# A decoder block's first stage: loading x first, and the modulation weights in four column quarters with projection weights between

## The chip, the cores and the metric

The kernel runs on one core of one Trainium2 chip. The metric is the time of one launch in microseconds (us) as the device takes it. All rows below are from one profiled execution, which took 1054.42 us; its trace spans 1052.4 us of them.

## What is computed

One layer of a hybrid decoder on 512 tokens of width 1024, in float32. Only its first lines matter here:

```python
ada = jax.nn.silu(c) @ w_ada + b_ada                 # c: 1024, w_ada: 1024 x 6144
shift1, scale1, gate1, shift2, scale2, gate2 = split(ada, 6)
h = rms_norm(x, norm1_g) * (1 + scale1) + shift1     # x: 512 x 1024
proj = h @ w_in                                      # 1024 x 3656, the columns in groups
```

From `proj` come a gated short convolution and a sparse attention with an indexer, then an output projection, and then a mixture of 64 experts over the 512 tokens, which takes most of the time.

## The kernel before, in words

The program is written out in the order in which each engine takes its instructions; nothing reorders them afterwards. An engine that waits holds up everything behind it.

**Shift and scale.** They need columns 0 to 2047 of `w_ada`, 8 MB, as eight row chunks k of 128 rows. `load_wa` (L114) puts row chunk k with all 2048 columns, 1 MB, into one of six buffers R0 to R5; the eighth comes in two column halves (`load_wa_half`, L124). `ada1(k)` (L185) is VectorE's product of one such chunk: `acc1 += wa[k] * silu(c)[k]`, 128x2048, so eight of them make the whole sum over this axis. TensorE then sums `acc1` over the partitions, 128 columns at a time (L356), and gives columns of shift and scale.

**x.** Four token blocks b of 128 tokens (0.5 MB each) are loaded in turn with the weight chunks. `norm1_sq` and `norm1` (L248, L253) run on ScalarE (square with sum, scaling) and TensorE (transposes, L260), with two copies by ScalarE (L83) per block, and leave x transposed in `xnT`, in eight chunks k of 128 columns by 512 tokens.

**Modulation.** `modulate(k0, n)` (L352) does it for n chunks: TensorE's L356 on `acc1`, three small sums on VectorE (L357, L358, L360), then for each chunk ScalarE writes `hh` (the rounded high part, L363), VectorE the full value into `xnT` (L364) and the low part `hl` (L365).

**Projection.** The loop over steps i (L1060) goes through 7 groups of 512 columns by 8 chunks k. A weight tile of a step, 128x512, is split by `split(i)` (L323) in two: ScalarE writes the high part into a `ring` tile (L83), VectorE the low part (L315). Each step then has three matmuls (L86 to L88) for each of four banks. In group 0 the first bank is left out, and `kw_mm` (L498) puts three products of a further weight, `kws`, in its place. `raw` tiles of 512 KB (two steps each) are loaded six steps ahead, and steps are split three ahead (`LOOK`). The fourth buffer of `raw` is one half of a tile named `both`.

**What runs beside it.** The other four parts of `ada` are summed on the way by `ada_item` (L388): a 512 KB chunk of `w_ada` (`both`, `adaw`) is scaled by ScalarE (L83, 128x1024) and added by POOL (L396). One is due at steps 1, 2, 4, 6, 8 and so on. `rope_tables` (L195) makes small tables for the positions, and its first instruction converts the positions to float (`posf`, L196). `at(i, f)` (L472, called from L947 on) puts f ahead of step i.

All large loads are issued by SP in program order. Each waits until the load eight before it has landed, and until its buffer has been read.

Of the kernel before, what the change touches and what calls it, by code (L numbers as in the profile page):

```python
# [13 lines left out]
F32R = mybir.dt.float32r  # L14
# [3 lines left out]
OP = mybir.AluOpType  # L18
# [32 lines left out]
def build(tc, a, out):  # L51
    nc = tc.nc
    root = ExitStack()
    with root:
# [12 lines left out]
        def M(tag, shape, name, dt=F32):  # L67
            return mem.tile(shape, dt, name=name, tag=tag)
# [33 lines left out]
        posi = M("q1", [NB, P], "posi", I32)  # L102
# [5 lines left out]

        wada = a["w_ada"][0].rearrange("(k p) n -> p k n", p=P)
        xv = x2d.rearrange("(b p) d -> p b d", p=P)  # L110
        wa = []
        xt = [M("A6", [P, 2, D], "xt0"), M("A7", [P, 2, D], "xt1")]

        def load_wa(k):  # L114
            t = M(f"R{k % 6}", [P, 2 * D], f"wa{k}")
            if k < KC - 1:
                nc.sync.dma_start(t, wada[:, k, 0:2 * D])
            wa.append(t)

        def wa_half(t, g):  # L120

            return t.rearrange("p (a d) -> p a d", a=2)[:, :, 512 * g:512 * g + 512]

        def load_wa_half(g):  # L124
            nc.sync.dma_start(wa_half(wa[KC - 1], g), wa_half(wada[:, KC - 1, 0:2 * D], g))

        def load_x(b):
            nc.sync.dma_start(xt[b // 2][:, b % 2], xv[:, b])

        for b in range(NB):  # L130
            load_wa(b)
            load_x(b)
        for k in (4, 5):
            load_wa(k)
        nc.scalar.dma_start(svR[16:32], a["b_ada"][:, 0:2 * D].rearrange("o (k p) -> (o k) p", p=P))
        nc.scalar.dma_start(svR[8:16], a["norm1_g"].rearrange("o (k p) -> (o k) p", p=P))
        nc.scalar.dma_start(svR[32:44], a["conv_w"].rearrange("o i (k p) -> (o i k) p", p=P))
# [34 lines left out]
        sc = small(KC)  # L172
# [12 lines left out]
        def ada1(k, g=None):  # L185
            if k == 0:
                nc.vector.tensor_scalar(acc1, wa[k], sc[:, 0:1], None, op0=OP.mult)
            else:
                v = [wa[k], acc1] if g is None else [wa_half(t, g) for t in (wa[k], acc1)]
                nc.vector.scalar_tensor_tensor(v[1], v[0], sc[:, k:k + 1], v[1], op0=OP.mult, op1=OP.add)  # L190


        posf = M("q0", [NB, P], "posf")

        def rope_tables():  # L195
            nc.vector.tensor_copy(posf, posi)  # L196
            nc.tensor.transpose(K6[:, 0, :NB], posf, ident[:NB, :NB])
            posT = small(NB)
            nc.vector.tensor_copy(posT, K6[:, 0, :NB])
# [63 lines left out]
        ada1(0)
        ada1(1)
        load_wa(6)
        load_wa(7)
        load_wa_half(0)
        norm1_sq(0)
        for b in range(NB):
            if b + 1 < NB:  # L270
                norm1_sq(b + 1)
            norm1(b)
            ada1(b + 2)
            if b == 1:
                vectors()
        sin = cos = None

        def rope_build():
# [62 lines left out]
        ada1(7, 0)
        split(0)

        def split_kw():
            kwf = [t.rearrange("p k n -> p (k n)") for t in (kwr, kws[:, 0], kws[:, 1])]
            copy_a(kwf[1], kwf[0])
            nc.gpsimd.tensor_tensor(kwf[2], kwf[0], kwf[1], op=OP.subtract)
# [17 lines left out]
                nc.vector.tensor_sub(l, x, h)  # L365

        modulate(0, 1)
        ada1(7, 1)
        split(1)
        modulate(1, 3)  # L370
        split(2)
        split_kw()


        acc2 = M("B1", [P, 2, D], "acc2")
# [96 lines left out]
        def at(i, f, *args):  # L472
            hooks.setdefault(i, []).append((f, args))
# [470 lines left out]
            mods7 = M("A7", [P, 2, D], "mods7")  # L944
            bcast_rows(mods7[:, 1], a["norm2_g"], D)

        at(1, modulate, 4, 2)  # L947
        at(4, rope_build)
        at(2, modulate, 6, 2)
        at(8, qi_done)  # L950
        at(8, kw_done)
        at(9, kw_T)
# [107 lines left out]
        for i in range(NS):  # L1060
            for f, args in hooks.pop(i, []):
                f(*args)
            g, k = divmod(i, KC)
            if i + 6 < 8 * NG:
                load_step(i + 6)
            if g < NG:
                split_step(i + LOOK if i + LOOK < 8 * NG else NS)
# [8 lines left out]
            if g < NG:  # L1076
                t = splits.pop(i)
                for j in range(4):
                    fill(i, r + (1.2 if j == 0 and k == 0 else 0))
                    if g == 0 and j == 0:  # L1080
                        for kk in {0: (), 1: (), 7: (5, 6, 7)}.get(k, (k - 2,)):
                            kw_mm(kk)
                    elif g < 4:
                        mm3(banks[j], hh[k // 4][:, k % 4, j * P:(j + 1) * P], hl[k // 4][:, k % 4, j * P:(j + 1) * P],
                            t[:, 0], t[:, 1], k == 0, k == KC - 1)
                    else:
                        mm3(banks[j], t[:, 0, j * P:(j + 1) * P], t[:, 1, j * P:(j + 1) * P], hh[k // 4][:, k % 4],
                            hl[k // 4][:, k % 4], k == 0, k == KC - 1)
# [885 lines left out]
```

## Time and profile before

| what | us |
|---|---|
| median of 3 runs (1052.13 to 1064.34) | 1053.35 |
| the profiled execution | 1054.42 |
| its span in the trace | 1052.4 |
| TensorE busy | 912.7 |
| VectorE busy | 531.4 |
| ScalarE busy | 270.5 |
| POOL busy | 391.6 |

The change touches about the first 75 us. There the trace is read by stretches (which engine is busy), then by the instructions of one engine in order of time, each with the idle time before it and what ended that.

### The profile page before, as it was taken

The numbers are of one execution on the slowest core, as the hardware profiler recorded it, in microseconds if no ns is written. First come the engines' busy times: TensorE is split into PE (matmuls) and PEld (weight loads), VectorE is DVE, ScalarE is ACT, GpSimd is POOL, SyncE is SP. The second block draws the span as 40 slices with busy tenths as digits, with TensorE's granted clock in tenths as the row PEclk, the third lists the DMA queues.
The fourth block names the chain that finished last, engine by engine and source line by source line (L and its number), as shares of the span: only waits on it lengthen the run. The fifth ranks groups of instructions, "written<-read, shape, count | busy, mean of one in ns | idle before, by whom it ended". The sixth has DMA issues, their size and how long they took to land. (4 is left out here: it accounts for less than half of the span.)

```text
span 1052.4 us, 14840 instructions
## 1 busy us (share of the span) xinstructions
PE 912.7 (87%) x4156; PEld 535.2 (51%) x4157; DVE 531.4 (50%) x1299; ACT 270.5 (26%) x527; POOL 391.6 (37%) x402
## 2 busy tenths in 40 slices
PE   1788989899998889788999989999998888889883
PEld 1666556566666767554444434444444444444341
DVE  4865976677756887734233434333233333333331
ACT  4544545544354442020000101111111111111110
POOL 3254688443534555332122323223232323333331
PEclk9989989899999989999999999999999999999987
DMA  9544232332523766695699996888988788889621
GB/s 336 196 162 158 88 128 86 121 100 80 180 92 109 278 223 230 202 329 177 195 298 317 278 346 229 286 274 297 308 293 301 260 288 267 294 258 373 158 33 27
DMA packets 71288, 227.80 MB, mean 216 GB/s; under 512 B 11858, under 2 KB 13010, under 8 KB 70208
## 3 DMA queue, kind: packets, MB, share of 16 engines
q1 hardware_dynamic: 55512, 189.90, 50.3%
q0 software_dynamic: 15520, 35.72, 14.9%
q8 instruction: 80, 1.31, 0.5%
q14 instruction: 104, 0.85, 0.2%
q10 hardware_dynamic: 72, 0.02, 0.0%
HBM read 207.75 MB, written 27.39 MB: 223 GB/s over the span
## 5 line engine op out<-in xcount | busy, mean ns | idle before, releaser
L1715 PE MATMUL pAB<-w,xT 128*128 128x512 f32 (+2 forms) x928 | 300.2, 609 | 18.8 <-ACTq L1878 5.7
L1715 PEld LDWEIGHTS pAB<-w,xT 128*128 128x128 f32 (+2 forms) x928 | 122.9, 160 | 154.0 <-issue 133.1
L1167 POOL DMA_INDIRECT out_dram<-ysb,misc x38 | 60.8, 1599 | 210.9 <-DVE ysb L1161 98.5
L1782 PE MATMUL pY<-w,q2u 128*128 128x512 f32 x256 | 116.4, 598 | 5.8 <-issue 4.1
L83 ACT ACTIVATE xT<-pX 128x512 f32<-128x512 f32 x59 | 35.1, 596 | 207.7 <-PE pX L1661 207.6
L1469 POOL DMA_INDIRECT X<-h_d,misc x51 | 54.2, 1063 | 84.6 <-DVE misc L1443 32.2
L1167 POOL DMA_INDIRECT out_dram<-y,misc x20 | 31.7, 1585 | 131.6 <-DMA out_dram<-ysb,misc 28.8
L1161 DVE SCALAR_TENSOR_TENSOR ysb<-pY,misc,gate 128x512 f32<-128x512 f32 x56 | 39.5, 746 | 70.7 <-DMA out_dram<-ysb,misc 31.7
L1782 PEld LDWEIGHTS pY<-w,q2u 128*128 128x128 f32 x256 | 46.5, 192 | 53.9 <-issue 51.9
L1454 DVE TENSOR_REDUCE rd<-pI 128x4 f32<-128x12 f32 (+1 forms) x45 | 7.6, 168 | 118.7 <-PE pI L1451 118.6
L315 POOL TENSOR_TENSOR ring<-raw,ring 128x512 fp32r<-128x512 f32 x29 | 38.4, 1323 | 70.2 <-ACT ring L83 70.2
L86 PE MATMUL Z<-ring,hh 128*128 128x512 f32 x120 | 56.3, 469 | 0.0
L87 PE MATMUL Z<-ring,hh 128*128 128x512 f32 x120 | 50.9, 424 | 0.0
L88 PE MATMUL Z<-ring,hl 128*128 128x512 f32 x120 | 50.9, 424 | 0.0
L396 POOL TENSOR_TENSOR acc<-acc,both 128x1024 f32<-128x1024 f32 x16 | 38.4, 2401 | 32.1 <-ACT both L83 22.7
L83 ACT ACTIVATE ring<-raw 128x512 fp32r<-128x512 f32 x66 | 41.3, 627 | 34.1 <-PE Z L88 30.3
L315 DVE TENSOR_TENSOR ring<-raw,ring 128x512 fp32r<-128x512 f32 x37 | 41.3, 1124 | 17.3 <-ACT ring L83 15.7
L86 PE MATMUL Z<-hh,ring 128*128 128x512 f32 x96 | 44.5, 463 | 0.0
L396 POOL TENSOR_TENSOR acc<-acc,adaw 128x1024 f32<-128x1024 f32 x16 | 39.1, 2446 | 14.1 <-DVE cy L629 7.5
L1788 PE MATMUL pY<-w,q2u 128*32 128x256 f32 (+1 forms) x360 | 33.9, 419 | 11.2 <-issue 8.0
L1446 DVE TENSOR_SCALAR gts<-sl,pu 128x256 bf16<-128x256 bf16 x180 | 41.5, 301 | 1.6
L1661 PE MATMUL pX<-ident,X 128*128 128x128 f32 x268 | 40.6, 289 | 0.0
(452 smaller groups left out, 1600.9 us busy)
## 6 DMA issues: line engine op xcount, KB each, us to landing
w<-in_w_dram SPq DMA_DIRECT2D x164, 512.0 KB
w<-in_w_dram SPq DMA_DIRECT2D x41, 1024.0 KB
raw<-in_w_in_dram SPq DMA_DIRECT2D x21, 512.0 KB
both<-in_w_ada_dram SPq DMA_DIRECT2D x16, 512.0 KB
adaw<-in_w_ada_dram SPq DMA_DIRECT2D x16, 512.0 KB
wa<-in_w_ada_dram SPq DMA_DIRECT2D x7, 1024.0 KB
raw<-in_w_out_dram SPq DMA_DIRECT2D x12, 512.0 KB
both<-in_w_in_dram SPq DMA_DIRECT2D x7, 512.0 KB
```

The lines of the kernel that those rows point to most:

```text
L83: nc.scalar.activation(o, i, AF.Copy, **kw)
L86: nc.tensor.matmul(p, lh, rh, start=start, stop=False)
L87: nc.tensor.matmul(p, lh, rl, start=False, stop=False)
L88: nc.tensor.matmul(p, ll, rh, start=False, stop=stop)
L315: eng.tensor_tensor(t[:, 1], r, t[:, 0], op=OP.subtract)
L396: eng.tensor_tensor(t, t, w, op=OP.add)
L1167: nc.gpsimd.indirect_dma_start(out=parts(acc_d, k), out_offset=bass.IndirectOffsetOnAxis(ap=idx, axis=0), in_=y[:, 0:D // k], in_offset=No ...
L1446: nc.vector.tensor_scalar(selx[:, b], sl2, pu[:, b, u:u + 1], None, op0=OP.is_equal)
L1469: nc.gpsimd.indirect_dma_start(out=xg[:, 0:D // k], out_offset=None, in_=parts(h2_d, k), in_offset=bass.IndirectOffsetOnAxis(ap=idx, axis= ...
L1661: nc.tensor.transpose(pX[c // 4][:, c % 4], x[:, c * P:(c + 1) * P], ident)
L1715: nc.tensor.matmul(ab[r * m:r * m + r], x[:, c, r * m:r * m + r], slot(v, cw // 4)[:, :, cw % 4], start=c == 0, stop=c == KC // k - 1)
L1782: nc.tensor.matmul(pY[n], q2[:, i, c], slot(w, 2)[:, c, 512 * n:512 * n + 512], start=c == 0, stop=c == 1)
```

## The change

x is loaded ahead of all weights. The 8 MB of shift and scale are cut by columns: `load_wa(g)` loads quarter g, that is 256 columns of shift and the 256 of scale that belong to them, for all eight row chunks, in eight loads of 256 KB with rows of 1 KB. `ada1(g)` is then eight products of 128x512, and after it chunks 2g and 2g+1 can be modulated. The weights of `kws` are loaded after quarter 1 was used (`load_kw`), in a buffer that quarter 1 had, and split at step 4; their products move to steps 5 to 7. `posf` is converted at the start, and `rope_build` moves from step 4 to step 6.

```diff
-        for b in range(NB):
-            load_wa(b)
-            load_x(b)
-        for k in (4, 5):
-            load_wa(k)
+        def load_wa(g):
+            for n in range(4 * g, 4 * g + 4):
+                if n % 2 == 0:
+                    t = M(f"R{n // 2 % 6}", [P, 2, 2, 2, 256], f"wa{n}")
+                    wa[n], wa[n + 1] = t[:, 0], t[:, 1]
+                for i in range(2):
+                    nc.sync.dma_start(wa[n][:, i], quarter(wada[:, 2 * (n % 4) + i, 0:2 * D], g))
+        for b in range(NB):
+            nc.sync.dma_start(xt[b // 2][:, b % 2], xv[:, b])
+        load_wa(0)
...
+        def ada1(g):
+            t = quarter(acc1, g)
+            for k in range(KC):
+                w = wa[4 * g + k // 2][:, k % 2]
+                if k == 0:
+                    nc.vector.tensor_scalar(t, w, sc[:, 0:1], None, op0=OP.mult)
+                else:
+                    nc.vector.scalar_tensor_tensor(t, w, sc[:, k:k + 1], t, op0=OP.mult, op1=OP.add)
+        nc.vector.tensor_copy(posf, posi)
...
         load_ahead(0)
-        load_wa_half(1)
-        nc.sync.dma_start(kwr, win[:, :, 3584:3656])
-        for i in range(2, 6, 2):
-            load_ahead(i)
-        ada1(6)
-        ada1(7, 0)
+        load_wa(1)
+        load_ahead(2)
+        load_wa(2)
+        load_wa(3)
+        load_ahead(4)
         split(0)
...
         modulate(0, 1)
-        ada1(7, 1)
+        modulate(1, 1)
         split(1)
-        modulate(1, 3)
+        ada1(1)
         split(2)
-        split_kw()
+        load_kw()
+        load_ahead(6)
...
-        at(1, modulate, 4, 2)
-        at(4, rope_build)
-        at(2, modulate, 6, 2)
+        at(2, modulate, 2, 2)
+        at(2, ada1, 2)
+        at(4, modulate, 4, 2)
+        at(4, ada1, 3)
+        at(4, split_kw)
+        at(6, modulate, 6, 2)
+        at(6, rope_build)
...
-                        for kk in {0: (), 1: (), 7: (5, 6, 7)}.get(k, (k - 2,)):
+                        for kk in {5: (0, 1), 6: (2, 3), 7: (4, 5, 6, 7)}.get(k, ()):
```

The order on three engines shows what stands behind what. Numbers at the names are those of buffers, and the square brackets hold the engines or the DMA slots that a row waits for.

SP before, from the second half of the last chunk (`wa_149`) to the first weights of the other parts (`both` from `in_w_ada`):

```order
L125 DMA wa_149<-in_w_ada_dram 128x2x512 [waits DMAHW1_49]
L337 DMA kwt<-in_w_in_dram 128x8x72 [waits DMAHW2_49,DVE_49]
L310 DMA raw_220<-in_w_in_dram 128x2x512 [waits DMAHW3_49]
L310 DMA raw_222<-in_w_in_dram 128x2x512 [waits DMAHW4_49]
L401 DMA acc_264<-in_b_ada_dram 1x1024 [waits DMAHW5_49,Activation_49,Pool_49]
L383 DMA both<-in_w_ada_dram 128x1024 [waits DMAHW6_49]
```

SP of the change, from the last load of quarter 3 (`wa_240`):

```order
L125 DMA wa_240<-in_w_ada_dram 128x2x256 [waits DMAHW1_49]
L302 DMA raw_245<-in_w_in_dram 128x2x512 [waits DMAHW2_49]
L336 DMA kwt<-in_w_in_dram 128x8x72 [waits DMAHW3_49,DVE_49]
L302 DMA both<-in_w_in_dram 128x2x512 [waits DMAHW4_49,Pool_49]
L398 DMA acc_283<-in_b_ada_dram 1x1024 [waits DMAHW5_49,Activation_49,Pool_49]
L380 DMA both<-in_w_ada_dram 128x1024 [waits DMAHW6_49]
```

`kwt` now stands behind all four quarters, and its wait for VectorE is for the last product of quarter 1; a `raw` load (`both` from `in_w_in`) has moved in between it and the weights of the other parts.

ScalarE before, around its first scaling of such weights (`both<-both`), with the `hh` of chunks 4 to 7 around it:

```order
L363 ACTIVATE hh_141<-xnT_139,sm_77 128x512 [waits DVE_49,Activation_49]
L363 ACTIVATE hh_141<-xnT_139,sm_77 128x512
L83 ACTIVATE ring_304<-raw_222 128x512 [waits DMAHW4_49,PE_49,Activation_49]
L83 ACTIVATE both<-both,sm_77 128x1024 [waits DMAHW6_49]
L363 ACTIVATE hh_141<-xnT_139,sm_77 128x512 [waits DVE_49]
```

The same place of the change, where the `hh` rows ahead of it are chunks 0 and 1 and those behind it are chunks 2 and 3:

```order
L359 ACTIVATE hh_139<-xnT_137,sm_77 128x512 [waits DVE_49,Activation_49]
L359 ACTIVATE hh_139<-xnT_137,sm_77 128x512 [waits DVE_49]
L83 ACTIVATE ring_266<-raw_211 128x512
L83 ACTIVATE ring_277<-raw_223 128x512 [waits DMAHW1_49]
L83 ACTIVATE ring_309<-raw_245 128x512 [waits DMAHW2_49,PE_49,Activation_49]
L83 ACTIVATE both<-both,sm_77 128x1024 [waits DMAHW6_49]
L359 ACTIVATE hh_139<-xnT_137,sm_77 128x512 [waits DVE_49]
```

Before, two chunks (6 and 7) were modulated behind that scaling; now six are.

VectorE of the change, from chunk 3 (end of step 2's modulation) to the sums for chunks 4 and 5. Before, nothing but two or three rows of L315 stood between two modulations:

```order
L361 TENSOR_TENSOR hl_141<-xnT_137,hh_139 128x512
L185 TENSOR_SCALAR acc_133<-wa_225,sm_77 128x2x256
L187 SCALAR_TENSOR_TENSOR acc_133<-wa_225,sm_77,acc_133 128x2x256 x3
L187 SCALAR_TENSOR_TENSOR acc_133<-wa_230,sm_77,acc_133 128x2x256 x4
L307 TENSOR_TENSOR ring_347<-raw_245,ring_347 128x512
L307 TENSOR_TENSOR ring_363<-both,ring_363 128x512
L353 TENSOR_TENSOR sm_77<-side_127,sm_77 128x2
```

Quarter 2's eight products have moved between chunk 3 and chunk 4; quarter 3's stand likewise between chunk 5 and chunk 6.

## Rows read from the trace of the kernel before

**Rows 1.** Stretches: busy us (instructions) of each engine, PE clock, DMA share, GB/s.
```profile
20.00:25.00 5.00, 2.23 (x9) 1.75 (x9) 3.31 (x3) 3.54 (x8) 0.82 (x3) 1.00 1.03 425
30.00:35.00 5.00, 3.19 (x15) 2.73 (x14) 3.88 (x6) 2.10 (x4) 0.00 (x0) 1.00 1.10 352
53.90:58.40 4.50, 0.26 (x2) 0.04 (x1) 4.37 (x5) 0.10 (x1) 2.07 (x1) 0.84 0.90 289
...
58.40:71.30 12.90, 12.90 (x46) 9.46 (x47) 6.57 (x15) 4.75 (x7) 9.79 (x22) 0.79 0.26 85
```

**Rows 2.** TensorE in order of time: start, us, line; first and last product of group 0.
```profile
36.95 0.77 PE L86 MATMUL Z<-ring,hh 128*128 128x512 f32 x1
...
58.36 0.26 PE L197 MATMUL K<-ident,posf 4*128 4x4 f32 x1 [4.24 <-DVE posf L196]
58.56 0.70 PE L498 MATMUL K<-hh,kws 128*72 128x512 f32 x1
...
63.32 0.60 PE L88 MATMUL Z<-ring,hl 128*128 128x512 f32 x1
63.75 0.41 PE L498 MATMUL K<-hh,kws 128*72 128x512 f32 x1
...
73.15 0.39 PE L88 MATMUL Z<-ring,hl 128*128 128x512 f32 x1
73.37 0.39 PE L86 MATMUL Z<-ring,hh 128*128 128x512 f32 x1
```

**Rows 3.** ScalarE in order of time: second square, last copy, first ring, first `hh`.
```profile
14.22 1.06 ACT L250 ACTIVATE scr<-xt 128x1024 f32<-128x1024 f32 x1 [5.68 <-DMA xt<-in_x_dram]
...
31.62 0.60 ACT L83 ACTIVATE xnT<-Z 128x512 f32<-128x512 f32 x1 [0.26 <-PE Z L260]
32.11 0.62 ACT L83 ACTIVATE ring<-raw 128x512 fp32r<-128x512 f32 x1
34.61 0.81 ACT L363 ACTIVATE hh<-xnT,sm 128x512 fp32r<-128x512 f32 x1 [1.88 <-DVE sm L360]
```

**Rows 4.** VectorE in order of time: its first product, of the first 1 MB.
```profile
6.09 1.29 DVE L187 TENSOR_SCALAR acc<-wa,sm 128x2048 f32<-128x2048 f32 x1 [2.69 <-DMA wa<-in_w_ada_dram]
```

**Rows 5.** VectorE in order of time: modulation of chunks 0, 4 and 5, and a 128x512 product.
```profile
34.09 0.16 DVE L357 TENSOR_TENSOR sm<-side,sm 128x1 f32<-128x1 f32 x1 [0.56 <-PE side L356]
...
36.03 0.69 DVE L365 TENSOR_TENSOR hl<-xnT,hh 128x512 fp32r<-128x512 f32 x1
...
46.97 0.55 DVE L364 TENSOR_SCALAR xnT<-xnT,sm 128x512 f32<-128x512 f32 x1 [0.95 <-ACT hh L363]
...
48.73 0.69 DVE L365 TENSOR_TENSOR hl<-xnT,hh 128x512 fp32r<-128x512 f32 x1
49.34 0.68 DVE L315 TENSOR_TENSOR ring<-raw,ring 128x512 fp32r<-128x512 f32 x1
49.94 0.15 DVE L357 TENSOR_TENSOR sm<-side,sm 128x2 f32<-128x2 f32 x1
...
160.22 0.75 DVE L562 SCALAR_TENSOR_TENSOR msk<-rel,sm,msk 128x512 f32<-128x512 f32 x1 [2.76 <-ACT rel L556]
```

**Rows 6.** VectorE, groups by shape, 0 to 60 us: busy us, mean ns, idle before.
```profile
L190 DVE SCALAR_TENSOR_TENSOR acc<-wa,sm,acc 128x2048 f32<-128x2048 f32 x6 | 14.1, 2352 | 9.3 <-DMA wa<-in_w_ada_dram 9.2
...
L190 DVE SCALAR_TENSOR_TENSOR acc<-wa,sm,acc 128x1024 f32<-128x1024 f32 x2 | 2.6, 1282 | 0.0
```

**Rows 7.** SP and ScalarE in order of time: the first load and scaling for other parts.
```profile
44.86 0.25 SPq L401 DMA_DIRECT2D acc<-in_b_ada_dram  x1
...
48.97 1.15 ACT L83 ACTIVATE both<-both,sm 128x1024 f32<-128x1024 f32 x1 [0.81 <-DMA both<-in_w_ada_dram]
50.39 1.52 ACT L363 ACTIVATE hh<-xnT,sm 128x512 fp32r<-128x512 f32 x2 [0.27 <-DVE sm L360]
```

**Rows 8.** POOL in order of time: the three long operations of 42 to 56 us.
```profile
42.29 1.65 POOL L347 TENSOR_TENSOR kws<-kwt,kws 128x576 fp32r<-128x576 f32 x1 [15.01 <-ACT kws L83]
...
50.25 2.40 POOL L396 TENSOR_TENSOR acc<-acc,both 128x1024 f32<-128x1024 f32 x1 [5.42 <-ACT both L83]
53.62 2.35 POOL L396 TENSOR_TENSOR acc<-acc,adaw 128x1024 f32<-128x1024 f32 x1 [0.97 <-ACT adaw L83]
```

**Rows 9.** VectorE in order of time, beside these.
```profile
42.69 1.80 DVE L365 TENSOR_TENSOR hl<-xnT,hh 128x512 fp32r<-128x512 f32 x1
...
51.24 1.70 DVE L364 TENSOR_SCALAR xnT<-xnT,sm 128x512 f32<-128x512 f32 x1 [0.89 <-ACT hh L363]
...
53.58 2.67 DVE L364 TENSOR_SCALAR xnT<-xnT,sm 128x512 f32<-128x512 f32 x1
```

**Rows 10.** Stretch with the lowest rate of loads, columns as in rows 1.
```profile
5.00:10.00 5.00, 0.00 (x0) 0.00 (x0) 1.29 (x1) 1.15 (x2) 1.94 (x5) 1.00 1.08 270
```

**Rows 11.** Stretches after group 0.
```profile
80.00:100.00 20.00, 16.64 (x75) 12.26 (x75) 12.87 (x29) 8.66 (x15) 11.52 (x9) 0.95 0.60 196
100.00:150.00 50.00, 48.34 (x164) 26.85 (x162) 40.74 (x88) 24.16 (x41) 34.85 (x31) 0.99 0.25 81
```

More of the change, by code (lines that the diff above doesn't have):

```diff
@@ L110, in build, with quarter @@
         xv = x2d.rearrange("(b p) d -> p b d", p=P)
-        wa = []
+        wa = {}
         xt = [M("A6", [P, 2, D], "xt0"), M("A7", [P, 2, D], "xt1")]
[L114 to L127, printed above, removed]
-            nc.sync.dma_start(xt[b // 2][:, b % 2], xv[:, b])
-        for b in range(NB):
-            load_wa(b)
-            load_x(b)
-        for k in (4, 5):
-            load_wa(k)
+        def quarter(t, g):
+            return t.rearrange("p (a d) -> p a d", a=2)[:, :, 256 * g:256 * g + 256]
+        def load_wa(g):
[6 more added lines that the diff above has]
+        for b in range(NB):
+            nc.sync.dma_start(xt[b // 2][:, b % 2], xv[:, b])
+        load_wa(0)
         nc.scalar.dma_start(svR[16:32], a["b_ada"][:, 0:2 * D].rearrange("o (k p) -> (o k) p", p=P))
@@ L183, in build @@
         cols = side[0][:, 0:2 * KC]
[L185 to L190, printed above, removed]
+        def ada1(g):
[6 more added lines that the diff above has]
+                    nc.vector.scalar_tensor_tensor(t, w, sc[:, k:k + 1], t, op0=OP.mult, op1=OP.add)
         posf = M("q0", [NB, P], "posf")
+        nc.vector.tensor_copy(posf, posi)
         def rope_tables():
-            nc.vector.tensor_copy(posf, posi)
             nc.tensor.transpose(K6[:, 0, :NB], posf, ident[:NB, :NB])
@@ L261, in norm1 @@
                 copy_a(xnT[g][:, :, b * P:(b + 1) * P], tp)
[L263 to L267, printed above, removed]
         norm1_sq(0)
@@ L272, in build @@
             norm1(b)
-            ada1(b + 2)
-            if b == 1:
-                vectors()
+        ada1(0)
+        vectors()
         sin = cos = None
@@ L330, in lo_pool, with load_kw @@
             return i >= 16 and i % 3 != 0
-        kwt = M("R3", [P, 3, KC, 72], "kwt")
-        kwr = kwt[:, 0]
-        kws = M("R4", [P, 2, KC, 72], "kws", F32R)
+        kwr = kws = None
         load_ahead(0)
-        load_wa_half(1)
-        nc.sync.dma_start(kwr, win[:, :, 3584:3656])
-        for i in range(2, 6, 2):
-            load_ahead(i)
-        ada1(6)
-        ada1(7, 0)
+        load_wa(1)
[3 more added lines that the diff above has]
+        load_ahead(4)
         split(0)
+        def load_kw():
+            nonlocal kwr
+            kwr = M("R3", [P, 3, KC, 72], "kwt")[:, 0]
+            nc.sync.dma_start(kwr, win[:, :, 3584:3656])
         def split_kw():
+            nonlocal kws
+            kws = M("R4", [P, 2, KC, 72], "kws", F32R)
             kwf = [t.rearrange("p k n -> p (k n)") for t in (kwr, kws[:, 0], kws[:, 1])]
@@ L1063, in build @@
             g, k = divmod(i, KC)
-            if i + 6 < 8 * NG:
+            if 0 < i < 8 * NG - 6:
                 load_step(i + 6)
```

## The prediction

> **What bounds the kernel now.** I read the table of stretches first, then TensorE in order of time, then the engines that it waits for. Up to about 35 us the loads set the pace: 425 GB/s from 20 to 25 us and 352 from 30 to 35, with TensorE nearly idle [rows 1]. The first product of group 0 starts at 36.95, and the first of group 1 at 73.37 [rows 2]. The nine matmuls per step and the 24 for `kws` make 96, which at the full clock (73.15 to 73.37, 0.22 to 0.23 each [rows 2]) would need 21.8 us. The stage takes 36.4. The largest gap is 53.9 to 58.4, where TensorE is busy 0.26 of 4.50 us and VectorE 4.37 [rows 1], and the row that ends it waits 4.24 us for `posf` on VectorE [rows 2]. After such a gap twelve products take 58.56 to 63.75, 0.43 each, the lower of the two clock levels [rows 2]. So from the moment that the loads are in, VectorE's order bounds this stage. All after it hangs on its end: group 1 uses the banks and the `hh` and `hl` that group 0 leaves. I therefore forecast when group 1 starts, and shift the rest by as much.
>
> **The change, part by part.**
>
> *x first.* The square of block 1 waits for x until 14.22 [rows 3]. The first 1 MB of the queue has landed at 6.09 [rows 4]; after the change that 1 MB is x blocks 0 and 1. The chain of squares, scalings, transposes and copies has 18.0 us from 14.22 to the last copy's end (31.62 + 0.60 [rows 3]), all of it ScalarE and TensorE waiting for each other, and it keeps that length. It moves by 14.22 - 6.09 = 8.1 us: the ring copy of step 0 starts at 32.11 - 8.1 = 24.0, its low part is done 1.4 later (0.62 and 0.69 [rows 3, 5]) at 25.4. Quarter 0 lies behind 4 MB of the queue, about 16 us, so its products are under the norm and cost nothing; without that cover they would cost 5.8, below.
>
> *The products in quarters.* A product has 2352 ns for 2048 columns and 1282 for 1024 [rows 6]. The line through both gives 0.75 us for 512, and an operation of this kind with 128x512 elsewhere has 0.75 [rows 5]. The first of a quarter is of the form of L364, 0.55 [rows 5]. A quarter is 0.55 + 7 x 0.75 = 5.8 us, and four are 23.2 against 18.0 before (1.3 + 14.1 + 2.6 [rows 4, 6]). The sum grows by 5 us; more important is that three quarters now stand between modulations.
>
> *Chunks 0 and 1.* One modulation takes VectorE 34.09 to 36.72, 2.63 us with its wait for `hh` [rows 5]. So chunk 0 is done at 28.0, chunk 1 at 30.7, the low part of step 1 (0.60 from start to start [rows 5]) at 31.3, and quarter 1, long landed, at 31.3 + 5.8 = 37.1. The first product would start near 26.5, ten us earlier than now. That is the gain of the change.
>
> *The load of `kws`.* SP holds `kwt` until 37.1, since it needs quarter 1's buffer, and behind it stand the fourth `raw` and the weights of the other parts. Now, the issue of the bias at 44.86 leads to the first scaling at 48.97, 4.1 us, with 0.5 MB to move [rows 7]. With `kwt` and a `raw` ahead, 0.84 million bytes more at 400 GB/s (between 352 and 425 [rows 1]) are 2.1 us. So the scaling starts at 37.1 + 4.1 + 2.1 = 43.3. ScalarE takes its work in order, and the `hh` of chunk 2 stands behind that scaling: 43.3 + 1.15 [rows 7] = 44.45. The sums for chunk 2 would have let it go at 37.1 + 3 x 0.60 + 0.45 = 39.4, so 5 us of the gain are lost here, and TensorE idles meanwhile. By now the head start is gone: the present kernel is at chunk 4 at 46.97 [rows 5], the changed one at chunk 2.
>
> *From chunk 2 to chunk 6.* VectorE is the chain: `hh` 0.81 [rows 3], then 46.97 to 49.42 for the rest of two chunks, 2.45 [rows 5]; the quarter, 5.8; two low parts of weights, 1.2; the sums, 0.45 (49.94 [rows 5] to 50.39 [rows 7]). That is 10.7 for a pair, twice, 21.4. POOL adds to it. While POOL has an operation of 1.65, 2.40 or 2.35 us [rows 8], VectorE's operation beside it takes 1.80, 1.70 and 2.67 instead of 0.69, 0.55 and 0.55 [rows 5, 9]: it ends only after POOL's does. Four such stand beside this chain (the first three additions and the split of `kws`): 3 x 2.4 + 1.65 = 8.8, of which 0.8 is under the first `hh`. Before, the three rows cost 4.4 us; the chain now is longer and has room for all four. At least it is 4.4 again, at most 8.8; I take 8.0, since VectorE hardly pauses. So `hh` of chunk 6 starts at 44.45 + 21.4 + 8.0 = 73.9.
>
> *The end of group 0.* After that `hh` (0.81) come nine products, twelve for `kws` and nine: 30 x 0.226 = 6.8 us. The six for `kws` ahead of them run while TensorE waits, and they are half of the twelve at the lower clock; the other six cost 6 x 0.2 = 1.2 more. Group 1 starts at 73.9 + 0.8 + 6.8 + 1.2 = 82.7, against 73.4: **9.3 us later**.
>
> *`posf` and the rope tables.* The early cast removes the wait of 4.24 us. It gives nothing here, as step 4 then waits for VectorE's quarter 2 instead. The ten small operations move behind chunk 7's modulation, where TensorE has 30 products of work; without that cover they cost 2.4 us.
>
> *Loads.* Rows become 1 KB and loads 256 KB. The trace has no such row. The nearest, 512 KB with rows of 2 KB, are in the stretch with 352 GB/s; the fastest stretch has 425 [rows 1], the slowest with loads queued 270 [rows 10]. All up to the first scaling is 13.4 million bytes. VectorE lets the last of it be issued so late that above 325 GB/s (13.4 in 41.3 us) nothing changes; at 270 it lands near 51.6, 8.3 us later. I take 352 or more, as it is nearest in shape. The Trainium skill speaks against such loads: "DMA: Bandwidth & Descriptors", section "Bandwidth", has a measured fit of 2.0 us plus the bytes at 436 GB/s for one load, and the rule to batch to 1 MiB or more. By it a load of 256 KB alone is 2.6 us, 32 of them 83 us, and the stage would end some 30 us later than now. No run here shows such loads; the stretch of 352 GB/s has half the batch that the rule asks for and several loads in flight.
>
> **The rivals.**
> 1. *Faster: the quarter's products are cheaper than the line says.* 21 of them are on the chain (quarters 1 to 3). At 0.30 us each instead of 0.75 the 9.3 us are gone; only below that is the kernel faster, at 0.25 about 1052. For it: nothing but that this pattern (two runs of 256) is not in the trace. Against it: 0.75 in the row of equal size [rows 5].
> 2. *The wait at chunk 2 is not there*, or POOL costs only 4.4 again: 5.0 or 3.6 us less, 1058 or 1059. For it: the landing of 43.3 hangs on four terms. Against: the order of both queues.
> 3. *Given back later.* TensorE idles 3.4 us from 80 to 100 and 1.7 from 100 to 150 [rows 11]. If a late start shrinks these waits, 5 us come back, 1058. Against: what ends them (splits, copies of `qi`) starts with group 1 as well.
> 4. *Loads much slower*, at 270 GB/s [rows 10]: 8.3 more, 1071. The point is 325 GB/s. The skill's fit belongs here, and would go beyond.
>
> **How the numbers follow.** The likeliest, 64%: 9.3 us on the profiled 1054.4 gives 1063.7; the median of the runs lies 1.1 lower, so 1063 us, with a range of its own of 1059 to 1068 (4.4 of POOL's cost, or a landing that is 3 us later). Rival 1 has 4%, rival 2 12% (1055 to 1059), rival 3 8% (1054 to 1059), rival 4 12% (1069 to 1085). The range 1054 to 1071 leaves out rival 1 and about half of rival 4. A measurement of this kernel tells 2% (21 us) from no change. That is beyond all but the tail of rival 4: slower by more 4%, faster by more 1%, within 2% 95%.
>
> **What would show it.** Right: first product near 26 to 27 us; ScalarE's first 128x1024 scaling near 43, with `hh` of chunk 2 right behind it and TensorE idle from about 34 to 45; eight operations of 0.55 and 0.75 us in each quarter; POOL's additions beside VectorE's operations of 2 us or more; group 1 near 83. Wrong: a quarter of 3 us or less, `hh` of chunk 2 near 40, POOL's additions that fall in VectorE's waits, or loads that still run at 50 us. If group 1 starts near 83 and the whole is not 9 us longer, the shift was given back, and the stretches to 240 us would show where.

## The result, and the profile of the changed kernel

The changed kernel is slower by about 1%, as forecast.

| | before | changed |
|---|---|---|
| median, us | 1055.7 (20 executions) | 1066.4 (20 executions) |
| lowest to highest, us | 1049.6 to 1064.3 | 1059.5 to 1076.4 |
| ratio, with its 95% interval | | 1.0106 (1.0082 to 1.0130), or 8.7 to 13.7 us |
| the profiled execution, us | 1054.4 | 1072.7 |
| TensorE's mean granted clock in it | 0.958 | 0.936 |

The profiled execution of the changed kernel is one of its longest, 6 us above its median, and its mean granted clock is the lowest of the 20. So of its 18 us the last ones are not in the median, and the traces of the experiments have to say which. The ratio, here and below, leaves out the few executions in a slower state and is not exactly that of the two medians, which lie 10.7 us apart.

The loads first. Columns are as in rows 1: length, busy us (instructions) of the five engines, PE clock, DMA share, GB/s.

```profile
20.00:25.00 5.00, 3.18 (x13) 2.68 (x13) 0.42 (x2) 3.29 (x5) 0.00 (x0) 1.00 1.10 355
30.00:35.00 5.00, 4.46 (x13) 3.17 (x11) 4.82 (x8) 0.75 (x2) 0.00 (x0) 1.00 1.10 348
40.00:45.00 5.00, 0.00 (x0) 0.00 (x0) 0.99 (x4) 1.73 (x3) 0.00 (x0) 0.50 0.81 302
```

The 256 KB loads with rows of 1 KB run at 355 GB/s where 1 MB loads with rows of 8 KB had 425 [rows 1]. From 40 to 45 us TensorE does nothing and its clock stands at the lower level.

TensorE in order of time: first product of group 0, first of chunk 2, first of group 1 (rows 2 of before), and the turning of the index queries (`natqi`) behind it.

```profile
26.76 0.80 PE L86 MATMUL Z<-ring,hh 128*128 128x512 f32 x1
...
45.81 0.79 PE L86 MATMUL Z<-ring,hh 128*128 128x512 f32 x1 [6.88 <-ACT hh L359]
...
83.64 0.39 PE L86 MATMUL Z<-ring,hh 128*128 128x512 f32 x1
...
92.15 0.60 PE L452 MATMUL K<-ident,natqi 128*128 128x128 f32 x4
96.99 1.09 PE L452 MATMUL K<-ident,natqi 128*128 128x128 f32 x4 [4.24 <-ACT qiT L83]
```

The start is 10.2 us earlier than before, and group 1 is 10.3 us later. ScalarE in order of time shows the pairs of chunks (2, 4, 6), and the ring copy and the scaling ahead of the first:

```profile
40.26 0.63 ACT L83 ACTIVATE ring<-raw 128x512 fp32r<-128x512 f32 x1 [9.50 <-DMA raw<-in_w_in_dram]
...
43.90 1.15 ACT L83 ACTIVATE both<-both,sm 128x1024 f32<-128x1024 f32 x1 [3.02 <-DMA both<-in_w_ada_dram]
44.96 1.50 ACT L359 ACTIVATE hh<-xnT,sm 128x512 fp32r<-128x512 f32 x2
...
60.12 1.52 ACT L359 ACTIVATE hh<-xnT,sm 128x512 fp32r<-128x512 f32 x2 [7.43 <-DVE sm L356]
...
74.15 1.52 ACT L359 ACTIVATE hh<-xnT,sm 128x512 fp32r<-128x512 f32 x2 [7.79 <-DVE sm L356]
```

VectorE between chunk 2 and chunk 6, and POOL beside it:

```profile
45.79 2.05 DVE L360 TENSOR_SCALAR xnT<-xnT,sm 128x512 f32<-128x512 f32 x1 [3.85 <-ACT hh L359]
...
48.48 2.59 DVE L360 TENSOR_SCALAR xnT<-xnT,sm 128x512 f32<-128x512 f32 x1
...
51.71 0.48 DVE L185 TENSOR_SCALAR acc<-wa,sm 128x512 f32<-128x512 f32 x1
52.23 5.47 DVE L187 SCALAR_TENSOR_TENSOR acc<-wa,sm,acc 128x512 f32<-128x512 f32 x7
...
62.73 1.79 DVE L361 TENSOR_TENSOR hl<-xnT,hh 128x512 fp32r<-128x512 f32 x1
64.45 2.59 DVE L185 TENSOR_SCALAR acc<-wa,sm 128x512 f32<-128x512 f32 x1
```

```profile
45.19 2.36 POOL L393 TENSOR_TENSOR acc<-acc,both 128x1024 f32<-128x1024 f32 x1 [25.60 <-ACT both L83]
48.16 2.62 POOL L393 TENSOR_TENSOR acc<-acc,adaw 128x1024 f32<-128x1024 f32 x1 [0.61 <-ACT adaw L83]
62.29 1.69 POOL L343 TENSOR_TENSOR kws<-kwt,kws 128x576 fp32r<-128x576 f32 x1 [11.50 <-DVE hl L361]
63.94 2.81 POOL L393 TENSOR_TENSOR acc<-acc,both 128x1024 f32<-128x1024 f32 x1
```

A quarter is 5.99 us (51.71 to 57.70). Four VectorE operations that stand beside one of POOL take 2.05, 2.59, 1.79 and 2.59 us instead of 0.55, 0.54, 0.69 and 0.48.

### The profile page after: what moved, and what is told of

It is laid out like the page before. It is cut to its first block, busy times and chain, and to the rows that moved or that the text cites. A ratio compares the mean times of both kernels' runs of the same rounds, so it can differ in the third digit from the quotient of the medians.

```text
span 1070.7 us, 14909 instructions
## 1 busy us (share of the span) xinstructions
PE 932.2 (87%) x4156; PEld 545.7 (51%) x4157; DVE 538.5 (50%) x1325; ACT 270.4 (25%) x527; POOL 392.3 (37%) x402
## 5 line engine op out<-in xcount | busy, mean ns | idle before, releaser
L1783 PE MATMUL pY<-w,q2u 128*128 128x512 f32 x256 | 122.3, 623 | 9.0 <-issue 3.4
L86 PE MATMUL Z<-ring,hh 128*128 128x512 f32 x120 | 59.0, 491 | 8.3 <-ACT hh L359 8.2
L88 PE MATMUL Z<-ring,hl 128*128 128x512 f32 x120 | 53.6, 447 | 1.8 <-DVE hl L361 1.6
L87 PE MATMUL Z<-ring,hh 128*128 128x512 f32 x120 | 53.5, 446 | 0.0
L307 DVE TENSOR_TENSOR ring<-raw,ring 128x512 fp32r<-128x512 f32 x37 | 38.2, 1041 | 19.2 <-ACT ring L83 17.3
L86 PEld LDWEIGHTS Z<-ring,hh 128*128 128x128 f32 x120 | 26.4, 220 | 28.9 <-issue 13.6
```

The costliest lines, as they stand in the source:

```text
L86: nc.tensor.matmul(p, lh, rh, start=start, stop=False)
L87: nc.tensor.matmul(p, lh, rl, start=False, stop=False)
L88: nc.tensor.matmul(p, ll, rh, start=False, stop=stop)
L307: eng.tensor_tensor(t[:, 1], r, t[:, 0], op=OP.subtract)
L1783: nc.tensor.matmul(pY[n], q2[:, i, c], slot(w, 2)[:, c, 512 * n:512 * n + 512], start=c == 0, stop=c == 1)
```

## The experiments

The table holds one profiled execution of each kernel (starts of group 1, of the first score and of the out projection, in us), and the ratio to the kernel before over its executions. One execution is a small sample: those of e6, e8 and e11 are the shortest of their kernel, that of e3 is the longest of its four.

| kernel | group 1 | first score | out proj. | ratio (95%) |
|---|---|---|---|---|
| before | 73.4 | 94.3 | 332.6 | |
| changed | 83.6 | 108.9 | 350.8 | 1.0106 (1.0082 to 1.0130) |
| e1 before, early `posf` | 66.4 | 94.1 | 330.6 | 0.9992 (0.9956 to 1.0027) |
| e2 changed, other parts later | 74.4 | 99.7 | 339.6 | 1.0072 (1.0034 to 1.0110) |
| e3 changed, `kwt` behind | 84.1 | 108.7 | 350.5 | 1.0107 (1.0055 to 1.0159) |
| e4 before, x first | 72.6 | 93.6 | 328.2 | 0.9973 (0.9945 to 1.0001) |
| e5 changed, tables early | 87.1 | 109.3 | 343.7 | 1.0105 (1.0019 to 1.0192) |
| e6 = e2 and e5 | 73.8 | 94.7 | 333.2 | 1.0036 (0.9995 to 1.0076) |
| e7 before, tables early | 76.0 | 96.9 | 334.3 | 1.0031 (0.9990 to 1.0071) |
| e8 = e7, x first | 75.2 | 96.1 | 330.5 | 1.0037 (0.9997 to 1.0077) |
| e9 before, tables in the first gap | 66.8 | 87.7 | 324.5 | 0.9955 (0.9924 to 0.9985) |
| e10 = e9, x first | 66.5 | 87.4 | 323.0 | 0.9973 (0.9943 to 1.0003) |
| e11 = e6, tables behind the norm | 73.9 | 94.8 | 334.5 | 1.0097 (1.0069 to 1.0125) |
| e12 = e11, gaps filled | 73.9 | 94.8 | 343.4 | 1.0036 (1.0001 to 1.0071) |

### The first group: e3 and e2

e3 puts the load of `kwt` behind the first two loads for the other parts:

```diff
         split(2)
-        load_kw()
         load_ahead(6)
...
         for n in range(2):
             ada_load(n)
+        load_kw()
```

> The changed kernel with the load of the kws weights moved behind the first two loads for the other parts. If SP's wait for quarter 1's buffer holds up the scaling ahead of chunk 2's hh (the step of the prediction), it starts near 40 instead of 43.9, and group 1 2 to 3 us earlier. If the loads themselves are late (raw2 landed at 40.26 in the trace of after, with the DMA engines busy throughout at 350 GB/s), it starts no earlier than 42.5 and group 1 moves by 1 us or less.

e2 lets the other parts' weights fall due from step 7 on:

```diff
-            ada_at.setdefault(1 + 7 * n // 4, []).append(n)
+            ada_at.setdefault(7 + 6 * n // 4, []).append(n)
```

> The changed kernel, with the sums for the other parts of ada (scaling by ScalarE, addition by POOL) due from step 7 on instead of from step 1, so that neither stands in group 0. If the scaling ahead of chunk 2's hh and POOL's additions beside VectorE cost what the trace of after shows (44.96 instead of about 42.0 for that hh, and 2.05, 2.59 and 2.59 us instead of about 0.5 for three operations), hh of chunk 2 starts at 42 and group 1 near 75 instead of 83.6, and the whole is about 8.5 us below the changed kernel, close to the kernel before. If the quarters alone set the chain, group 1 stays at 81 or later.

SP in order of time, first in the changed kernel, then in e3:

```profile
33.54 0.37 SPq L302 DMA_DIRECT2D raw<-in_w_in_dram  x1
37.04 0.37 SPq L336 DMA_DIRECT2D kwt<-in_w_in_dram  x1
...
38.45 0.34 SPq L380 DMA_DIRECT2D both<-in_w_ada_dram  x1
```

```profile
34.17 0.37 SPq L302 DMA_DIRECT2D raw<-in_w_in_dram  x1
...
36.45 0.34 SPq L379 DMA_DIRECT2D both<-in_w_ada_dram  x1
...
37.98 0.38 SPq L336 DMA_DIRECT2D kwt<-in_w_in_dram  x1
```

The hold at 37.04 is real, and in e3 the weights of the other parts are issued 2.0 us earlier. But there the scaling starts at 43.44 instead of 43.90, and the `hh` of chunk 2 at 44.49 instead of 44.96: half a microsecond. Issued at 36.45, the load takes 7.0 us to land; issued at 38.45, it took 5.5. The queue ahead of it is what it waits for, and a `raw` tile issued at 33.54 lands only at 40.26. So two bounds, the hold and the loads, lie within 0.5 us of each other, and to take one away uncovers the other.

In e2 the scaling and POOL's additions are gone from group 0. ScalarE there:

```profile
42.06 1.52 ACT L359 ACTIVATE hh<-xnT,sm 128x512 fp32r<-128x512 f32 x2 [1.09 <-DVE sm L356]
...
52.87 1.52 ACT L359 ACTIVATE hh<-xnT,sm 128x512 fp32r<-128x512 f32 x2 [4.57 <-DVE sm L356]
...
64.77 1.52 ACT L359 ACTIVATE hh<-xnT,sm 128x512 fp32r<-128x512 f32 x2 [5.96 <-DVE sm L356]
```

Chunk 2 is 2.9 us earlier. It is not at 39.4, where the prediction had it without the scaling: the `raw` tile lands late as in the changed kernel (its copy starts at 40.33), and its split stands ahead of chunk 2's sums. Chunk 6 follows 22.7 us behind chunk 2 instead of 29.2. Of these 6.5 us, 5.7 are the three rows of VectorE that stood beside POOL's additions. The other 0.8 are TensorE's column sums for chunk 4, shown here first in the changed kernel, where the granted clock was 0.50, then in e2, where it was 1.00:

```profile
57.76 1.87 PE L352 MATMUL side<-sm,acc 128*128 128x1 f32 x8 [2.79 <-DVE acc L187]
```

```profile
51.32 1.05 PE L352 MATMUL side<-sm,acc 128*128 128x1 f32 x8 [1.13 <-DVE acc L187]
```

Group 1 starts at 74.4, as expected, only 1.0 us later than before. But the ratio stays at 1.0072, so a second loss lies behind group 1. The first score, which came 20.9 us behind group 1 before, comes 25.3 behind it here and 25.2 in the changed kernel.

### The second loss: e5 and e6

The changed kernel from 79.7 to 97 us, POOL, SP and ScalarE:

```profile
80.05 0.26 POOL L228 TENSOR_TENSOR rtab<-sm 128x32 f32<-128x32 f32 x1 [13.30 <-ACT sm L214]
...
85.92 0.28 POOL L233 TENSOR_SCALAR rtab<-rtab 128x32 f32<-128x32 f32 x1
86.17 2.38 POOL L393 TENSOR_TENSOR acc<-acc,adaw 128x1024 f32<-128x1024 f32 x1
88.62 2.40 POOL L393 TENSOR_TENSOR acc<-acc,both 128x1024 f32<-128x1024 f32 x1
```

```profile
88.57 0.33 SPq L380 DMA_DIRECT2D adaw<-in_w_ada_dram  x1
```

```profile
79.72 0.26 ACT L214 ACTIVATE sm<-rt 128x64 f32<-128x64 f32 x1 [4.05 <-DVE rt L212]
...
92.58 1.15 ACT L83 ACTIVATE adaw<-adaw,sm 128x1024 f32<-128x1024 f32 x1 [4.34 <-DMA adaw<-in_w_ada_dram]
...
96.26 0.58 ACT L83 ACTIVATE qiT<-K 128x512 f32<-128x512 f32 x1
```

This is a chain through five queues. The sine on ScalarE (L214) waits for VectorE's ten small operations, and ScalarE stands idle for 4.05 us ahead of it; POOL makes the rope tables from 80.05 to 86.20, behind the sine, and only then adds; the buffer comes free and SP issues its next load at 88.57; ScalarE waits 4.34 us for it; the copy of the turned queries stands behind that; TensorE waits 4.24 us for the copy, and takes its next products at the lower clock (granted 0.50 from 97 to 101.5; 0.63 to 0.78 instead of 0.39 us).

In e5 and e6 VectorE's part of the tables runs at the start (the first `next`), and the sine and POOL's part behind quarter 1:

```diff
         def rope_tables():
...
+            yield
             nc.scalar.activation(trig, rr, AF.Sin)
...
-            return t4[:, 0], t4[:, 1]
+            yield t4[:, 0], t4[:, 1]
+
+        tables = rope_tables()
+        next(tables)
...
-            sin, cos = rope_tables()
+            sin, cos = next(tables)
...
         load_kw()
         load_ahead(6)
+        rope_build()
...
-        at(6, rope_build)
```

> The changed kernel, with the rotation tables made early: their VectorE part (11 small operations, 2.3 us, at 77.4 us in the changed kernel) stands at the start, where VectorE waits for the first weights (5.9 to 12.8 us), and their sine and the 20 small operations on POOL (4.9 us of POOL's time, ending at 86.2 us in the changed kernel) behind the second quarter's product. Nothing is left out. Theory (the changed kernel loses a second time behind the first column group, because the tables stand ahead of two 2.4 us additions on POOL, so that the buffer of the next weights comes free late, its load lands late, ScalarE waits 4.3 us for it, and the copy of the turned index queries stands behind that on ScalarE): TensorE's wait of 4.2 us for that copy is under 2 us, and the first score stands 20 to 22 us behind group 1's start, where it stood 25.2 us behind it; group 1 at 82 to 84 us; time 4 to 6 us below the changed kernel, 1060 to 1063 us. Rival (the tables don't matter, the additions are late by themselves because they are due every 1.75 steps): the wait stays at 4 us, the first score at 25 us behind group 1's start, time 1065 to 1068 us.

> The changed kernel with both edits: the other parts' weights due six steps later, and the rotation tables made early as in e5. Nothing is left out. Theory: group 1 starts at 73 to 75 us as in the run with the later due times alone, and the first score 20 to 22 us behind it, at 94 to 97 us, as in the kernel before (94.3 us): time within 3 us of the kernel before, ratio 0.998 to 1.004. So the two together account for the whole loss. Rival (tables don't matter): first score at 99 to 100 us, ratio 1.005 to 1.010.

What TensorE waits for up to the first score (line waited for: us, times, longest), in the kernel before, in the changed kernel and in e5:

```profile
PE K L455 <- ACT qiT L83: 1.9, 1, 1.9
```

```profile
PE K L452 <- ACT qiT L83: 4.2, 1, 4.2
```

```profile
PE K L457 <- ACT qiT L83: 1.9, 1, 1.9
```

The wait shrinks to 1.9, as in before, and the first score stands 22.3 us behind group 1. But group 1 itself is 3.4 us later, so the first score is no earlier than in the changed kernel (109.3 and 108.9), and the ratio, of four executions with a wide interval, can't be told from it either: POOL's 20 small operations now stand beside quarter 1 (its seven products take 5.92 instead of 5.47) and ahead of POOL's clearing of the accumulator (L397), which SP waits for before the bias row and the weights of the other parts. These are issued at 40.72 instead of 38.45:

```profile
40.72 0.34 SPq L385 DMA_DIRECT2D both<-in_w_ada_dram  x1
```

e6 has both edits, and in its trace both losses are gone: group 1 at 73.8 and the first score at 94.7, within 0.4 us of before. The ratio of 1.0036 can't be told from 1, though the traced execution (1053.8 us) is the shortest of ten with a median of 1059.0. Both edits move VectorE's ten operations, the sine and POOL's twenty together, so what each of the three is worth was not tested.

### The same table in the kernel before: e1, e4, e7, e8, e9, e10

e1 is the kernel before with the cast of `posf` at the start:

```diff
         posf = M("q0", [NB, P], "posf")
+        nc.vector.tensor_copy(posf, posi)
         def rope_tables():
-            nc.vector.tensor_copy(posf, posi)
```

> The kernel before with one part of the change alone: posf is converted at the start. The theory of the prediction (VectorE's order bounds group 0, and the conversion stood behind modulations that POOL held up) expects that step 4's products follow step 3's at 54 instead of 58.5, that the clock stays at its upper level, and that group 1 starts at 66 to 67 instead of 73.4, so about 7 us less in all. A rival, that TensorE would wait for the low part of chunk 6 or 7 anyway, expects group 1 at 71 or later.

e4 is the kernel before with x ahead of all weights, in whole rows as they were:

```diff
         for b in range(NB):
-            load_wa(b)
             load_x(b)
-        for k in (4, 5):
+        for k in range(6):
             load_wa(k)
```

> The kernel before with x loaded ahead of the weights, which stay in row chunks. The last copy of the norm should end near 24 instead of 32.2, but the first product needs all weights and stays at 36 to 37.5, group 1 at 73 to 74, and the time within 1 us. If the norm's chain were what delays the first product, it would come 2 us or more earlier.

e1 takes the 4.2 us of [rows 2] away and wins 7.0 us at group 1, since the products behind that gap no longer run at the lower clock (granted 1.00 from 53 to 66 us; before, 0.50 from 58.4 to 63.5). At the first score 0.2 us are left. ScalarE in e1 shows where they went:

```profile
73.04 1.15 ACT L83 ACTIVATE both<-both,sm 128x1024 f32<-128x1024 f32 x1 [5.85 <-DMA both<-in_w_ada_dram]
```

It is the same chain: POOL is at its tables until 66.7, so the third addition and the load behind it are no earlier than before. TensorE's wait for the copy of the turned queries is 4.1 us in e1, where before had 1.9.

e7 has e1's cast and e5's parting of the tables, and the rest of them ahead of step 0; e8 is e7 with e4:

```diff
         split_kw()
+        rope_build()
...
-        at(4, rope_build)
```

> The kernel before with the rotation tables made early (cast of the positions and VectorE's part at the start, sine and POOL's part behind the splitting of the index weights, ahead of step 0's products). Nothing is left out. Theory: with the cast alone group 1 came 7 us earlier (66.4 us) but the first score did not, since POOL's tables at 61 to 67 us held two additions, and ScalarE waited 5.9 us for the load that follows them; with the tables early both are gone: group 1 at 65 to 67 us, first score 20 to 23 us behind it, at 86 to 89 us, time 5 to 8 us below the kernel before, ratio 0.992 to 0.996. Rival (the additions on POOL or the loads are late by themselves): first score at 92 to 95 us, ratio 0.997 to 1.002.

> The kernel of e7 with x loaded ahead of all weights too. Nothing is left out. Loading x first alone gave 0.8 us at group 1's start and a ratio of 0.997 (0.9945 to 1.000). Theory: the two add up: group 1 at 64 to 66 us, first score at 85 to 88 us, ratio 0.988 to 0.995. Rival (the gain of x first was only spread): the same time as e7.

e7 was meant to remove that chain, and failed. SP, POOL and ScalarE in e7:

```profile
51.23 0.94 POOL L405 MEMSET acc<- 128x1024 f32 x1
```

```profile
52.20 0.25 SPq L406 DMA_DIRECT2D acc<-in_b_ada_dram  x1
52.50 0.34 SPq L388 DMA_DIRECT2D both<-in_w_ada_dram  x1
```

```profile
56.30 1.15 ACT L83 ACTIVATE both<-both,sm 128x1024 f32<-128x1024 f32 x1 [8.15 <-DMA both<-in_w_ada_dram]
```

The tables stood ahead of the clearing, which went from 43.9 to 51.2 us, and SP's bias row from 44.86 [rows 7] to 52.20. ScalarE's row says that it waits 8.15 us for a DMA; what is late is a MEMSET of 0.94 us on POOL. e8 has the same fault, at 75.2.

e9 is e7 with `rope_build` at another place, and e10 is e9 with e4:

```diff
         norm1_sq(0)
+        rope_build()
```

> The kernel before with the rotation tables made in the gap at the very start: VectorE's part from 5.9 us, the sine and the 20 operations of POOL behind the first row chunk's square, where POOL is idle from 9.5 to 15.5 us. Nothing is left out. In e7 they stood ahead of POOL's clearing of the accumulator, which went from 43.9 to 51.2 us; the bias row is loaded into that accumulator by SyncE's queue, so the next loads stood behind the clearing and landed 7.3 us late. Theory: without that the clearing is back at 43.9 us, group 1 starts at 65 to 67 us, as with the cast alone (66.4), and the first score stands 20 to 22 us behind it, at 85 to 89 us; time 4 to 8 us below the kernel before, ratio 0.992 to 0.997. Rival (something else gives the 7 us back, as in the run with the cast alone): first score at 92 to 95 us, ratio 0.998 to 1.002.

> The kernel of e9 with x loaded ahead of all weights too. Nothing is left out. Theory: group 1 at 64 to 67 us, first score at 84 to 88 us, ratio 0.989 to 0.996, with 0 to 3 us from x first. Rival: the first weights now land 4 us later and VectorE's first product with them, so that TensorE's start slips by 1 to 3 us: ratio 0.996 to 1.000.

Here the same work stands where VectorE and POOL are idle, from 7 us on, and the clearing is back at 44.1. Group 1 starts at 66.8, the first score at 87.7, 20.9 us behind it, and the ratio is 0.9955 (0.9924 to 0.9985), about 4.7 us faster than the kernel before. That is the lowest ratio here, though the intervals of e4 and e10 overlap with it. x first adds nothing that can be told from noise: 0.8 us at group 1 in e4, 0.3 in e10.

### What stays open: e11 and e12

e11 is e6 with `rope_build()` right behind the last `norm1`, ahead of the splitting of weights. e12 is e11 with products that nobody reads, ahead of the column sums and behind them:

```diff
+        def keep_busy(n):
+            for _ in range(n):
+                nc.tensor.matmul(K6.rearrange("p a b -> p (a b)"), hh[0][:, 0, 0:P], hh[0][:, 0], ...)
         def modulate(k0, n):
+            keep_busy({2: 12, 4: 8}.get(k0, 0))
...
+            keep_busy({2: 10, 4: 6}.get(k0, 0))
```

> The changed kernel with the other parts' weights due six steps later, and with the sine and POOL's part of the tables behind the norm of the last row chunk, ahead of POOL's clearing but at a time (about 24 to 29 us) when nothing waits for it. Nothing is left out. Theory: as e6, where group 1 started at 73.8 us and the first score stood 20.9 us behind it (94.7 us), or up to 2 us better: ratio 0.998 to 1.004. That would say that the loss of the changed kernel lies in its due times and in the place of the tables, and not in the quarters' order itself. Rival (the tables at POOL slow VectorE's second quarter product and add it to the chain of the scales): group 1 at 75 to 77 us, ratio 1.005 to 1.009.

> The kernel of e11 with 36 products whose sum nobody reads, put where TensorE waits in the first column group: 12 ahead of chunk 2's column sums and 10 behind them, 8 and 6 at chunk 4's (0.23 us each at the full clock, 2.3 to 2.8 us for the larger two, in gaps of 3.4, 3.8, 2.0 and 1.4 us). They add work and change no result. Why: in e11's profiled execution group 1 (73.9 us), the first score (94.8) and the end stand where the kernel before has them, and that execution is 1051.8 us, but the median of its 8 executions is 1061.0 us, with mean granted clocks of 0.938 to 0.960. In the executions of all kernels the time falls by about 7.7 us for each 0.01 of mean clock. Theory (the idle stretches of TensorE in group 0, with the clock at 0.5 to 0.8 in them, are what brings the lower mean clock, there and behind them): with the gaps filled the clock stands at 0.9 to 1.0 from 35 to 60 us, the median mean clock at 0.953 to 0.958 instead of 0.948, and the time 4 to 8 us lower, 1053 to 1057 us, ratio 1.001 to 1.005. Rival (the clock in group 0 and the rest have nothing to do with each other, or other stages decide it): group 0's clock rises and the time stays at a ratio of 1.008 to 1.012; or, with the gaps overfilled, up to 2 us more.

e11's trace keeps group 1 and the first score where before has them, and its profiled execution is 1051.8 us. Yet that is the shortest of its 8 executions; their median is 1061.0, with a median mean clock of 0.948 against 0.957 in before.

e11 and e9 were measured against the same executions of the kernel before, and both have the tables early. There e11 is 7.2 us behind e9 at group 1 and at the first score, and its ratio is 1.0097 against 0.9955. The changed kernel converts `posf` early, which e1 shows to be worth 7.0 us at group 1 in the old order. So the two repairs do not make the quarters free: they bring the changed kernel back to where the kernel before stood with its own wait for `posf`. (The due times of the other parts differ between e9 and e11 as well.)

e12 raises the median clock to 0.955, and its ratio is 1.0036 where e11 had 1.0097. That is what the theory wanted, but the two intervals touch at 1.007, so that the added products help is not shown. TensorE's stretches in e12 are these (columns as above):

```profile
35.00:60.00 25.00, 22.14 (x95) 16.73 (x93) 21.61 (x37) 6.56 (x10) 1.69 (x1) 0.93 0.57 191
...
94.80:120.00 25.20, 21.86 (x51) 11.05 (x50) 12.31 (x24) 9.40 (x19) 6.94 (x5) 0.66 0.25 84
```

Group 0 is at 0.93, and all the same the clock falls behind the first scores; the heads of `k` are turned 55.0 us behind the first score instead of 49.0. So that fall comes without idle stretches in group 0. Nor do they always bring it: in e5's trace the clock is 0.59 from 35 to 60 us and 1.00 in the 21 us behind the first score. The changed kernel's profiled execution has the fall too, and the kernel before hardly (columns as above, before second):

```profile
35.00:60.00 25.00, 11.30 (x34) 8.81 (x34) 17.23 (x26) 5.38 (x7) 4.98 (x2) 0.60 0.64 212
60.00:80.00 20.00, 16.35 (x54) 11.16 (x54) 17.12 (x33) 6.08 (x10) 4.47 (x2) 0.73 0.17 52
...
108.90:130.00 21.10, 19.64 (x44) 10.24 (x44) 9.88 (x17) 5.92 (x13) 4.77 (x3) 0.60 0.30 98
```

```profile
35.00:60.00 25.00, 18.47 (x73) 14.44 (x74) 20.86 (x39) 11.58 (x17) 7.28 (x4) 0.87 0.47 158
60.00:80.00 20.00, 20.00 (x84) 15.53 (x83) 11.46 (x23) 10.06 (x16) 14.42 (x26) 0.91 0.39 126
...
94.30:115.00 20.70, 18.93 (x60) 10.22 (x59) 13.63 (x24) 10.12 (x20) 8.70 (x5) 0.92 0.30 101
```

In which executions that fall comes, and why, no run here settles, nor where the other executions of e11 lose their 5 to 15 us.

## Why the prediction was right, and where its steps were not

**The direction, and the start of group 1: right.** 82.7 was forecast, 83.64 came.

- *x first and the first product:* 26.5 and 26.76.
- *A quarter:* 5.8 and 5.99. Rival 1 is out. 
- *Chunk 2:* 44.45 and 44.96, but the reason given for it was only part of it. The prediction had SP's hold for `kwt` as the cause, and loads fast enough not to matter ("above 325 GB/s nothing changes"). The loads came out just below that point: the seven stretches of 5 us from 5 to 40 move 11.6 MB (the first two at 246 and 327 GB/s), and the 13.4 million bytes are in at 43.9. That is 320 GB/s over 41.9 us, counted from 2 us on as the prediction's 41.3 us are. e3 shows that without the hold the loads alone give 44.49. And of the 5 us that the scaling was to cost, e2 shows 2.9; without it chunk 2 waits for the `raw` tile until 42.06. That 44.45 came so near is partly luck.
- *Loads:* the taken value of 352 GB/s for the running queue holds (348 to 358 from 15 to 35 us). The fit that the prediction took from the Trainium skill, "DMA: Bandwidth & Descriptors", stands there in the section "Anatomy of one DMA — SWDGE (gpsimd) path", not in "Bandwidth", and is for one load issued from GpSimd; here SP issues them. By the prediction's estimate from it, 32 such loads one after another, the stage would have ended some 30 us later. The trace disagrees with that use of it: with several loads in flight, 256 KB each, the rate is 82 to 84% of the 425 that 1 MB loads had.
- *Chunk 2 to chunk 6:* 29.4 was forecast (21.4 and 8.0 for POOL), 29.2 came. The four rows beside POOL cost 6.8 of the 8.0 (1.5, 2.1, 1.1 and 2.1). TensorE's column sums at the lower clock, which the prediction left out, add 0.8, and e2, with only the split of `kws` left, has 22.7. That the two nearly make up the 8.0 is luck.
- *The end of group 0:* 8.8 and 9.5.

**"I shift the rest by as much": the step that failed.** Between group 1 and the first score 4.3 us more are lost. The prediction costed the move of `rope_build` by its ten small operations on VectorE, found cover for them on TensorE and gave them nothing. It left out the sine, which waits for them on ScalarE, and the 20 small operations that the same call issues on POOL. With the additions queued behind them, they delay a buffer, a load, a scaling and a copy, one engine after the other. e5 brings the wait at its end back to 1.9, and e6, which is e5 and e2 together, brings both milestones back. The rival "given back later" looked only for gains there, not for a further loss.

Whether that rival came true as well stays open. e5's profiled execution is 15.0 us later than before at the first score and 11.1 at the out projection, so it takes 234.4 us from one to the other where before takes 238.3. But e4 and e8, whose first scores are at 93.6 and 96.1, also take some 234. A late start is not needed for the shorter stretch.

The early cast of `posf` was put at nothing, and at group 1 of this kernel that is right: TensorE waits 2.79 us for quarter 2 (57.76, above) instead. But e1 shows that the cast is worth 7.0 us in the old order. Against e1, group 1 of the changed kernel is 17.3 us later.

**The size.** 9.3 us were forecast, 11.2 came by the ratio (8.7 to 13.7). At the first score the profiled executions of the changed kernel, e3 and e5 are 14.4 to 15.1 us late, which is more. Why the executions as a whole lose less than that, no run shows. So that the whole came out near the forecast is in part luck: it left out a loss of 4.3 us, and something that is not known makes up for most of it. The profiled execution's further 7 us (18.3 in all) come with the fall of the clock from 108.9 to 130 us, 0.60 against 0.92: at the turning of `k`'s heads it is 20.6 us late, 6.0 more than at the first score.

**The mean clock.** Its median is 0.945 in the changed kernel and 0.956 in 81 executions of before. From 35 to 80 us the rows above miss 15.4 us of full clock in the changed kernel (25 x 0.40 and 20 x 0.27) and 5.1 in before; the 10.3 between them are 0.010 of the span. If group 0 is alike in all executions, nearly all of that difference lies there, where TensorE waits anyway: then it comes with the loss and is no second cause. e11, whose group 0 is much better, has nearly as low a median clock, and speaks against that being all.

## What to carry to other kernels

Follow everything that a moved call issues, on every engine. Twenty 0.25 us operations on an engine that looks idle, with the sine and the ten operations ahead of them, cost 4 us here, by way of a queue, a buffer, a load and a copy, and in e7 they cost more than the wait they were meant to remove. Small work with early inputs belongs in a gap where nothing stands behind it on its engine. And to win time at one milestone is not enough: e1 won 7 us at group 1 and lost nearly all of it 28 us later, because what paced the next stage had not moved.

## What the runs showed of the hardware that was not expected

- Loads with rows of 1 KB, 256 KB each and several in flight, run at 348 to 359 GB/s from 15 to 35 us in seven traces (the changed kernel, e2, e3, e5, e6, e11, e12), where rows of 8 KB and 1 MB loads have 415 to 433 from 15 to 25 us in the other seven. Loads of 512 KB with rows of 2 KB, from 30 to 35 us in those, have 352 to 353, no more than the shorter rows. The DMA share of the stretch reads 1.09 to 1.10 with either of the shorter rows, and 1.00 to 1.03 with the long ones.
- An engine's row names what came last and not what is late: 8.15 us of "DMA" in e7 are a clearing on POOL that moved by 7.3 us.
- Executions of one kernel differ by 10 to 20 us, and their time goes with the mean granted clock, by about 7.7 us for each 0.01 in 81 executions of the kernel before.
